# Projecting the queries of the band attention token by token, beside its keys and values

## The chip, the cores and the metric

The kernel runs on one core of a Trainium2 chip. The metric is the time of one execution on the device, in microseconds (us). Before the change three runs took 1618.82, 1613.80 and 1618.34 us, with a median of 1618.34.

## What is computed

One layer of a hybrid encoder, for 2048 prompt frames and 32 frames of a running stream, all in float32:

```python
h = rmsnorm(x, norm_gain)
qa, ka, va, ga, qb, kb, vb, gb = split(h @ w_in)        # 8 x 512 columns
oa = band_attention(qa, ka, va, rel_bias)                # A: 8 heads x 64, own chunk of 64 frames and 8 before
ob = subnorm(diff_attention(rope(qb), rope(kb), vb))     # B: 4 heads of two q/k pairs, block-causal over all frames
y  = rmsnorm(x + concat(oa * silu(ga), ob * silu(gb)) @ w_out, final_gain)
```

Keys and values of the last 512 frames (A) or of all frames (B) are outputs too, as are the rows of the running stream.

## The kernel before

The work is cut into eight **units** of 128 columns of each of q, k, v and gate: four of A (two heads each) and four of B (one head each). They run in the order A, B, B, A, B, A, B, A (line 695). Each unit runs over eight **chunks** of 256 frames (two row tiles of 128). Units on end share nothing but the normalised input, which lies transposed in device memory and is loaded per chunk (tile hT).

Every number is kept as a pair of rounded halves, so that a product is three matmuls: high by high, high by low, low by high. There are two ways to project. `project` (lines 292 to 298) is token-major: 128 frames of hT stand in the array as weights, the columns of w_in stream through, and the result has one frame per partition. `project_T` (lines 300 to 305) has the weights in the array and streams 256 frames: its result is already transposed, one column of w_in per partition. Both take 8 x 3 matmuls. A token-major result is scaled by the frame's norm, a per-partition number in rsd, in the same ACT instruction that takes it out of PSUM (line 349). A transposed result needs the scales along the row: tile rb, 128 equal rows of 256 scales, made in the first unit and loaded by DMA in the others (line 261).

A chunk of **B** projects q, k and v together token-major (384 columns), rotates q and k, and transposes k and q on TensorE (lines 370 and 372) into one PSUM tile tp. A chunk of **A** before the change projects only k and v so (256 columns, twice 24 matmuls), transposes k, and projects q with `project_T` (24 matmuls of 256 columns) into its own PSUM tile qp, which DVE multiplies by rb in place (line 353). From there both go the same way: ACT copies k and q into high parts (lines 382 to 389) and DVE subtracts for the low parts (lines 384 to 391). The gate of both is projected with `project_T` (line 395) and multiplied by rb (line 331). The scores (lines 425 and 426) then go through softmax on DVE, ACT and POOL, are transposed in blocks (line 434), split (lines 443 and 444) and multiplied with the values (lines 547 to 549 and 602 to 603). After the units, the output projection (line 792) uses `project` with 512 columns.

PSUM has two buffers for projections (z_ps), two for transposes (t_ps), three for scores (s_ps), one for outputs (o_ps). The order of the instructions on each engine is fixed when the program is built: a scheduler goes by a modelled timeline and by the priorities that `ahead(n)` gives. TensorE (PE), like the other engines, takes its instructions in that order.

The functions that the change touches are rb_tile, chunk_qkv and subnorm.

Of the kernel before, what the change touches and what calls it, by code (L numbers as in the profile page):

```python
# [8 lines left out]
F32 = mybir.dt.float32  # L9
# [5 lines left out]
P = 128  # L15
# [15 lines left out]
def hybrid_step(  # L31
# [79 lines left out]
    def z_psum():  # L111
        return psum.tile([P, 512], F32, name="z_ps", tag="z", bufs=2)
# [124 lines left out]
    def rb_tile():  # L237
        return pool.tile([P, 256], F32, name="rb", tag="rb", bufs=2)

# [102 lines left out]
    def chunk_qkv(u, isB, c, hR, W, kss, vts):  # L342
        hT, rb = hR
        z = pool.tile([P, 2, 384], F32, name="z", tag="z", bufs=2)
        z0 = 0 if isB else 128
        for tt in range(2):
            zp = z_psum()
            project(hT, tt, W, zp[:, z0:384], slice(z0, 384))
            ACT.activation(z[:, tt, z0:384], zp[:, z0:384], AF.Copy, scale=rsd[:, 2 * c + tt:2 * c + tt + 1])
        if not isB:  # L350
            qp = z_psum()
            project_T(hT, W, qp[:, 0:256], slice(0, 128))
            DVE.tensor_tensor(qp[:, 0:256], qp[:, 0:256], rb, ALU.mult)
        i = u % 4
# [12 lines left out]
        with ahead(150):  # L367
            tp = t_psum()
            for tt in range(2):
                PE.transpose(out=tp[:, tt * P:(tt + 1) * P], in_=z[:, tt, 128:256], identity=ident)  # L370
                if isB:
                    PE.transpose(out=tp[:, 256 + tt * P:256 + (tt + 1) * P], in_=z[:, tt, 0:128], identity=ident)
            if c % 2 == 0:
                kss.append(pool.tile([P, 2, 512], F32R, name="ks", tag="ks", bufs=5))
            ks = kss[c // 2][:, :, (c % 2) * 256:(c % 2 + 1) * 256]
            tk = tp[:, 0:256]
            tq = tp[:, 256:512] if isB else qp[:, 0:256]
            par = parity[0]
# [80 lines left out]
    def subnorm(ob, n, src=None):  # L459
        sq = pool.tile([P, 256], F32, name="sq", tag="sq", bufs=1)  # L460
        op, vp = ob[:, 0:n] if src is None else src, ob[:, 256:256 + n]
        ACT.activation(sq[:, 0:n], op, AF.Square)
        PE.matmul(vp, onesd, sq[:, 0:n], start=True, stop=True)
        rs = pool.tile([P, 256], F32, name="rs", tag="rs", bufs=1)
        ACT.activation(rs[:, 0:n], vp, AF.Ln, bias=eps_t)
        ACT.activation(rs[:, 0:n], rs[:, 0:n], AF.Exp, scale=-0.5)
        on = pool.tile([P, 256], F32, name="on", tag="on", bufs=1)
        DVE.scalar_tensor_tensor(on[:, 0:n], op, gcol[:, 0:1], rs[:, 0:n], ALU.mult, ALU.mult)
        return on
# [400 lines left out]
```

## Time and profile before

| | us |
|---|---|
| three runs, median | 1618.34 |
| the profiled execution, its own time | 1614.23 |
| its span (first to last instruction) | 1612.4 |
| PE busy | 1547.1 |
| DVE busy | 1093.3 |
| ACT busy | 1007.2 |
| POOL busy | 669.3 |

Busy time is the union of an engine's instructions. Matmuls overlap in the pipeline, so the duration of one is longer than what it adds: that is the distance between the starts of neighbours. The clock granted to TensorE was 0.99 of full speed on average. In this trace the units begin (first eviction of their first projection) at 18.5, 159.7, 326.4, 516.7, 699.9, 864.4, 1048.9 and 1214.7 us, in the order given above; the output projection follows from 1400 us on.

### The profile page before, as it was taken

The page shows a single profiled execution, that of the slowest core. Times are in us where ns is not written, and L with a number is a line of the kernel's source. Part 1 is how long each engine was busy: PE and PEld are TensorE (multiplying, and loading weights), DVE is VectorE, ACT ScalarE, POOL GpSimd, SP SyncE. Part 2 cuts the span into 40 slices and gives each one's busy share as a digit, 9 for nine tenths or more (in the row PEclk, how much of TensorE's full clock was granted, in tenths as well). Part 3 has the DMA queues.
Part 4 walks back from the last instruction along what each step waited for, and adds up shares of the span by engine and source line. Part 5 has one row for each costly group of instructions (what it writes and reads, how often), then busy time and mean ns, then how long its engine had stood idle before and what let it go on. Part 6 is the DMA issues. An engine that isn't in the chain of part 4 may idle for free.

```text
span 1612.4 us, 30675 instructions
## 1 busy us (share of the span) xinstructions
PE 1547.1 (96%) x10448; PEld 1430.0 (89%) x10448; DVE 1093.3 (68%) x3045; ACT 1007.2 (62%) x2706; POOL 669.3 (42%) x1117
## 2 busy tenths in 40 slices
PE   7999999999999899999998999999999999989997
PEld 7999999898998899999997999999878899968885
DVE  5777668885788856675788667666888577743333
ACT  7885667785778766655777566556677566531111
POOL 5565424653346534353446344443454344510000
PEclk9999999999999999999999999999999999999999
DMA  9964454433432153336422453354331264334562
GB/s 363 367 231 166 158 192 138 155 107 131 149 128 88 70 196 131 137 131 211 167 83 76 148 181 132 134 180 152 136 131 70 89 248 142 128 133 162 175 211 66
DMA packets 105662, 249.67 MB, mean 155 GB/s; under 512 B 11192, under 2 KB 60480, under 8 KB 88064
## 3 DMA queue, kind: packets, MB, share of 16 engines
q1 hardware_dynamic: 105504, 247.70, 43.3%
q8 instruction: 83, 1.36, 0.3%
q14 instruction: 75, 0.61, 0.1%
HBM read 194.83 MB, written 53.75 MB: 154 GB/s over the span
## 4 chain that ended last, share of the span: by engine, by line
PE 80%; DVE 9%; ACT 4%; issue 3%; DMA 3%; POOL 1%; SPq 0%; DVEq 0%; ACTq 0%; POOLq 0%
PE z_ps L296 12%; PE z_ps L297 12%; PE z_ps L298 12%; PE t_ps L434 6%; PE z_ps L303 5%; PE s_ps L425 5%; PE z_ps L304 5%; PE z_ps L305 5%; PE s_ps L426 5%; PE o_ps L603 2%; PE o_ps L602 2%; DVE nmx L513 2%; PE o_ps L547 2%; PE o_ps L548 2%; PE o_ps L549 2%
## 5 line engine op out<-in xcount | busy, mean ns | idle before, releaser
L296 PE MATMUL z_ps<-w,hT 128*128 128x256 f32 (+2 forms) x1280 | 424.0, 332 | 12.4 <-ACT w L179 6.2
L297 PE MATMUL z_ps<-w,hT 128*128 128x256 f32 (+2 forms) x1280 | 422.4, 330 | 2.0 <-DVE w L180 1.2
L298 PE MATMUL z_ps<-w,hT 128*128 128x256 f32 (+2 forms) x1280 | 421.2, 329 | 0.0
L296 PEld LDWEIGHTS z_ps<-w,hT 128*128 128x128 f32 x1280 | 243.5, 191 | 29.8 <-ACT w L179 6.2
L297 PEld LDWEIGHTS z_ps<-w,hT 128*128 128x128 f32 x1280 | 243.7, 190 | 18.5 <-DVE w L187 2.6
L298 PEld LDWEIGHTS z_ps<-w,hT 128*128 128x128 f32 x1280 | 243.7, 190 | 13.5
L515 ACT ACTIVATE e<-s_ps,nmx 128x512 f32<-128x512 f32 (+3 forms) x320 | 199.0, 626 | 85.1 <-DVE nmx L513 81.2
L444 DVE TENSOR_TENSOR pl<-t_ps,ph 128x512 fp32r<-128x512 f32 (+1 forms) x312 | 191.9, 622 | 77.2 <-ACT ph L443 66.4
L303 PE MATMUL z_ps<-hT,w 128*128 128x256 f32 x768 | 223.3, 291 | 2.8 <-DVE ql L391 2.2
L304 PE MATMUL z_ps<-hT,w 128*128 128x256 f32 x768 | 221.9, 289 | 0.0
L305 PE MATMUL z_ps<-hT,w 128*128 128x256 f32 x768 | 221.2, 288 | 0.0
L443 ACT CAST ph<-t_ps 128x512 fp32r<-128x512 f32 (+1 forms) x312 | 162.4, 535 | 91.2 <-PE o_ps L602 45.9
L425 PE MATMUL s_ps<-ks,qh 128*128 128x512 f32 (+2 forms) x544 | 193.5, 366 | 19.6 <-ACT e L515 17.6
L513 DVE TENSOR_REDUCE nmx<-s_ps 128x1 f32<-128x512 f32 (+3 forms) x320 | 188.2, 600 | 18.9 <-PE s_ps L426 16.0
L426 PE MATMUL s_ps<-ks,ql 128*128 128x512 f32 (+2 forms) x544 | 184.1, 351 | 0.0
L521 POOL TENSOR_SCALAR e<-e,da 128x512 f32<-128x512 f32 (+3 forms) x160 | 111.5, 711 | 140.8 <-DVE da L491 114.9
L303 PEld LDWEIGHTS z_ps<-hT,w 128*128 128x128 f32 x768 | 149.4, 194 | 6.5 <-DVE ql L391 2.9
L304 PEld LDWEIGHTS z_ps<-hT,w 128*128 128x128 f32 x768 | 149.5, 195 | 3.1 <-issue 1.3
L305 PEld LDWEIGHTS z_ps<-hT,w 128*128 128x128 f32 x768 | 149.5, 195 | 1.4
L580 POOL TENSOR_SCALAR ea<-ea,sma 128x640 f32<-128x640 f32 (+4 forms) x128 | 98.2, 769 | 112.8 <-DVE sma L579 99.5
L578 ACT ACTIVATE ea<-ea,nma 128x640 f32<-128x640 f32 (+4 forms) x128 | 97.2, 760 | 61.9 <-DVE nma L576 60.8
L425 PEld LDWEIGHTS s_ps<-ks,qh 128*128 128x128 f32 x544 | 101.8, 189 | 31.9 <-ACT e L515 25.2
(205 smaller groups left out, 3374.9 us busy)
## 6 DMA issues: line engine op xcount, KB each, us to landing
hT<-hTd SPq DMA_DIRECT2D x112, 1024.0 KB, 5.6
wraw<-in_w_in_dram SPq DMA_DIRECT2D x64, 256.0 KB, 5.2
hTd<-hT SPq DMA_DIRECT2D x8, 2048.0 KB, 8.9
oTd<-oT SPq DMA_DIRECT2D x64, 256.0 KB, 3.7
hT<-oTd SPq DMA_DIRECT2D x16, 1024.0 KB, 7.8
out_dram<-z SPq DMA_DIRECT2D x160, 64.0 KB, 1.6
xT<-in_x_t_dram SPq DMA_DIRECT2D x32, 256.0 KB, 5.2
xt<-in_x_prompt_dram SPq DMA_DIRECT2D x32, 256.0 KB, 6.0
```

The costliest lines, as they stand in the source:

```text
L296: PE.matmul(zp, hT[:, 0, k, ts], his[k][:, cols], start=(k == 0), stop=False)
L297: PE.matmul(zp, hT[:, 0, k, ts], los[k][:, cols], start=False, stop=False)
L298: PE.matmul(zp, hT[:, 1, k, ts], his[k][:, cols], start=False, stop=(k == KT - 1))
L303: PE.matmul(zp, his[k][:, cols], hT[:, 0, k, :], start=(k == 0), stop=False)
L304: PE.matmul(zp, his[k][:, cols], hT[:, 1, k, :], start=False, stop=False)
L305: PE.matmul(zp, los[k][:, cols], hT[:, 0, k, :], start=False, stop=(k == KT - 1))
L425: PE.matmul(sp[:, 0:w], QH[:, m, qs], ks[:, m, kc], start=True, stop=False)
L426: PE.matmul(sp[:, 0:w], QL[:, m, qs], ks[:, m, kc], start=False, stop=True)
L443: ACT.copy(out=hv, in_=tv)
L444: DVE.tensor_tensor(lv, tv, hv.bitcast(F32), ALU.subtract)
L513: DVE.tensor_reduce(nmx[:, m, b:b + 1], sp[:, 0:w], AX.X, ALU.max, negate=True)
L515: ACT.activation(e[:, 0:w], sp[:, 0:w], AF.Exp, bias=nmx[:, m, b:b + 1], accum_out=sm[:, m, b:b + 1])
```

## The change

A's q is projected token-major with k and v, as B's is: 384 columns in two times 24 matmuls, one ACT eviction of 384 columns for each row tile that scales all three. The 24 `project_T` matmuls of q and the DVE multiplication by rb go; two transposes for q come, into the second half of tp, and the copies and subtractions for q read them there instead of from qp. The row of scales gets a third buffer. Its space comes from the sub-norm of B, which keeps its result in the tile of squares instead of in one of its own.

```diff
     def rb_tile():
-        return pool.tile([P, 256], F32, name="rb", tag="rb", bufs=2)
+        return pool.tile([P, 256], F32, name="rb", tag="rb", bufs=3)
...
         z = pool.tile([P, 2, 384], F32, name="z", tag="z", bufs=2)
-        z0 = 0 if isB else 128
         for tt in range(2):
             zp = z_psum()
-            project(hT, tt, W, zp[:, z0:384], slice(z0, 384))
-            ACT.activation(z[:, tt, z0:384], zp[:, z0:384], AF.Copy, scale=rsd[:, 2 * c + tt:2 * c + tt + 1])
-        if not isB:
-            qp = z_psum()
-            project_T(hT, W, qp[:, 0:256], slice(0, 128))
-            DVE.tensor_tensor(qp[:, 0:256], qp[:, 0:256], rb, ALU.mult)
+            project(hT, tt, W, zp[:, 0:384], slice(0, 384))
+            ACT.activation(z[:, tt, :], zp[:, 0:384], AF.Copy, scale=rsd[:, 2 * c + tt:2 * c + tt + 1])
...
             for tt in range(2):
                 PE.transpose(out=tp[:, tt * P:(tt + 1) * P], in_=z[:, tt, 128:256], identity=ident)
-                if isB:
-                    PE.transpose(out=tp[:, 256 + tt * P:256 + (tt + 1) * P], in_=z[:, tt, 0:128], identity=ident)
+                PE.transpose(out=tp[:, 256 + tt * P:256 + (tt + 1) * P], in_=z[:, tt, 0:128], identity=ident)
...
-            tq = tp[:, 256:512] if isB else qp[:, 0:256]
+            tq = tp[:, 256:512]
...
-        rs = pool.tile([P, 256], F32, name="rs", tag="rs", bufs=1)
-        ACT.activation(rs[:, 0:n], vp, AF.Ln, bias=eps_t)
-        ACT.activation(rs[:, 0:n], rs[:, 0:n], AF.Exp, scale=-0.5)
+        ACT.activation(sq[:, 0:n], vp, AF.Ln, bias=eps_t)
+        ACT.activation(sq[:, 0:n], sq[:, 0:n], AF.Exp, scale=-0.5)
         on = pool.tile([P, 256], F32, name="on", tag="on", bufs=1)
-        DVE.scalar_tensor_tensor(on[:, 0:n], op, gcol[:, 0:1], rs[:, 0:n], ALU.mult, ALU.mult)
+        DVE.scalar_tensor_tensor(on[:, 0:n], op, gcol[:, 0:1], sq[:, 0:n], ALU.mult, ALU.mult)
```

The scheduler lays the whole program out anew; two places matter below.

**PE, the start of the program.** The end of the first chunk's projection (z_ps_246 and z_ps_272 are its two row tiles) and what follows. Before:

```order
L298 MATMUL z_ps_272<-w_176,hT_179 128x256
L253 MATMUL t_ps_218<-ident_67,rsd_92 128x128
L370 MATMUL t_ps_324<-ident_67,z_245 128x128
L303 MATMUL z_ps_298<-hT_179,w_155 128x256
L304 MATMUL z_ps_298<-hT_179,w_155 128x256
L305 MATMUL z_ps_298<-hT_179,w_155 128x256
```

With the change:

```order
L298 MATMUL z_ps_272<-w_176,hT_179 128x384
L253 MATMUL t_ps_218<-ident_67,rsd_92 128x128
L365 MATMUL t_ps_298<-ident_67,z_245 128x128
L366 MATMUL t_ps_298<-ident_67,z_245 128x128
L303 MATMUL z_ps_424<-hT_179,w_155 128x256
L304 MATMUL z_ps_424<-hT_179,w_155 128x256
L305 MATMUL z_ps_424<-hT_179,w_155 128x256
```

Before, the transposed projections that follow are q's 24 (z_ps_298), then the gate's 24. With the change the gate's come at once (z_ps_424); q is in the 48 matmuls above, each half as wide again.

**PE, the last chunk of the second A unit** (the fourth unit to run). The transposes of its k, and now of its q, and what stands around them. Before, z_ps_10164 is the chunk's q, still being projected when k is transposed:

```order
L303 MATMUL z_ps_10164<-hT_9874,w_7695 128x256
L370 MATMUL t_ps_10194<-ident_67,z_10111 128x128 x2
L603 MATMUL o_ps_9986<-pl_10043,vt_9372 128x256
L602 MATMUL o_ps_9986<-ph_10042,vt_9372 128x256
L603 MATMUL o_ps_9986<-pl_10043,vt_9372 128x256
L304 MATMUL z_ps_10164<-hT_9874,w_7695 128x256
```

With the change (z_ps_10077 is a projection of the next unit):

```order
L298 MATMUL z_ps_10077<-w_9832,hT_9805 128x384
L365 MATMUL t_ps_9790<-ident_67,z_9733 128x128
L366 MATMUL t_ps_9790<-ident_67,z_9733 128x128
L365 MATMUL t_ps_9790<-ident_67,z_9733 128x128
L366 MATMUL t_ps_9790<-ident_67,z_9733 128x128
L596 MATMUL o_ps_9608<-pl_9665,vt_9042 128x256
L595 MATMUL o_ps_9608<-ph_9664,vt_9042 128x256
L596 MATMUL o_ps_9608<-pl_9665,vt_9042 128x256
```

From the last transpose to the first score matmul that reads this chunk's q there now stand 9 projection matmuls of 384 columns, 2 score matmuls of the chunk before (256 columns), 7 value matmuls and 3 transposes. Before, 105 instructions lay between the two, among them the rest of q's projection and the gate's whole one.

## Rows read from the trace of the kernel before

**Rows 1.** The profile's page: busy time and share of each engine; then the mean busy share of the 16 DMA engines in tenths, in 40 slices of 40.3 us.

```profile
PE 1547.1 (96%) x10448; PEld 1430.0 (89%) x10448; DVE 1093.3 (68%) x3045; ACT 1007.2 (62%) x2706; POOL 669.3 (42%) x1117
...
DMA  9964454433432153336422453354331264334562
```

**Rows 2.** Busy time by window, in the middle of the four A units. Columns: window and its length; busy us (and instructions) of PE, PEld (weight loads), DVE, ACT, POOL; granted clock of PE; DMA share, GB/s.

```profile
40.00:160.00 120.00, 118.98 (x943) 115.10 (x943) 88.58 (x304) 93.41 (x260) 73.81 (x115) 1.00 0.69 257
600.00:690.00 90.00, 90.00 (x727) 87.75 (x726) 61.20 (x192) 56.31 (x140) 36.87 (x84) 1.00 0.39 141
950.00:1040.00 90.00, 90.00 (x727) 87.65 (x726) 60.09 (x194) 56.18 (x139) 36.40 (x85) 1.00 0.37 134
1300.00:1390.00 90.00, 90.00 (x725) 87.70 (x724) 66.14 (x205) 55.94 (x140) 41.05 (x90) 1.00 0.47 170
```

**Rows 3.** The same view, 20 us at each of the three changes from a B unit to an A unit.

```profile
500.00:520.00 20.00, 16.14 (x103) 12.98 (x102) 19.29 (x45) 16.49 (x48) 13.48 (x14) 1.00 0.42 152
845.00:865.00 20.00, 16.04 (x93) 12.18 (x92) 19.85 (x43) 16.20 (x46) 15.21 (x17) 1.00 0.42 155
1198.00:1218.00 20.00, 16.15 (x103) 12.99 (x102) 19.29 (x45) 16.50 (x48) 13.49 (x14) 1.00 0.45 152
```

**Rows 4.** The waits of PE over the whole span: who was waited for, us in total, times, longest us.

```profile
PE s_ps L425 <- ACT e L515: 17.6, 18, 2.5
PE z_ps L296 <- ACT w L179: 6.2, 1, 6.2
...
PE z_ps L303 <- DVE ql L391: 2.2, 2, 1.7
```

**Rows 5.** The timeline of PE: first and last matmul of four unbroken runs of projection matmuls. The runs have 24 (56.23 to 58.99) and 28 (634.71 to 638.02) matmuls of 256 columns, 24 and 24 of 384 columns. Columns: start, duration, instruction.

```profile
56.23 0.28 PE L296 MATMUL z_ps<-w,hT 128*128 128x256 f32 x1
...
58.99 0.28 PE L298 MATMUL z_ps<-w,hT 128*128 128x256 f32 x1
...
634.71 0.36 PE L296 MATMUL z_ps<-w,hT 128*128 128x256 f32 x1
...
638.02 0.28 PE L296 MATMUL z_ps<-w,hT 128*128 128x256 f32 x1
...
805.30 0.35 PE L296 MATMUL z_ps<-w,hT 128*128 128x384 f32 x1
...
809.30 0.34 PE L298 MATMUL z_ps<-w,hT 128*128 128x384 f32 x1
...
1067.33 0.42 PE L296 MATMUL z_ps<-w,hT 128*128 128x384 f32 x1
...
1071.43 0.34 PE L298 MATMUL z_ps<-w,hT 128*128 128x384 f32 x1
```

**Rows 6.** The chain that ended last, one piece of it in an A unit: start, us, what.

```profile
91.66 0.77 PE t_ps L434 x7
```

**Rows 7.** Groups of instructions by line and form, over the span: count, busy us in total, mean ns of one; then idle time before them and what ended it.

```profile
L349 ACT ACTIVATE z<-z_ps,rsd 128x384 f32<-128x384 f32 x64 | 37.0, 577 | 11.2 <-PE z_ps L298 10.9
L349 ACT ACTIVATE z<-z_ps,rsd 128x256 f32<-128x256 f32 x64 | 30.1, 470 | 18.9 <-PE z_ps L298 17.8 <-DVE rsd L203 0.5
...
L383 ACT CAST ks<-t_ps 64x256 fp32r<-64x256 f32 x64 | 23.5, 367 | 0.8
L386 ACT ACTIVATE qh<-z_ps 64x256 fp32r<-64x256 f32 x32 | 12.0, 375 | 13.4 <-DVE z_ps L353 13.1
...
L353 DVE TENSOR_TENSOR z_ps<-z_ps,rb 128x256 f32<-128x256 f32 x32 | 13.7, 429 | 10.2 <-PE z_ps L305 9.4
...
L372 PE MATMUL t_ps<-ident,z 128*128 128x128 f32 x64 | 15.9, 273 | 0.0
```

**Rows 8.** The timeline at the start of the program: PE from the end of the first chunk's token-major projection, and the first matmul of the second chunk's (27.62); POOL's low parts of the second chunk's input. In brackets: idle time before and what ended it.

```profile
16.60 0.28 PE L298 MATMUL z_ps<-w,hT 128*128 128x256 f32 x1
17.92 0.32 PE L253 MATMUL t_ps<-ident,rsd 128*128 128x128 f32 x1 [1.04 <-DVE rsd L203]
19.00 0.33 PE L370 MATMUL t_ps<-ident,z 128*128 128x128 f32 x1 [0.76 <-ACT z L349]
19.09 0.36 PE L303 MATMUL z_ps<-hT,w 128*128 128x256 f32 x1
...
26.73 0.52 PE L425 MATMUL s_ps<-ks,qh 128*128 128x256 f32 x3
...
27.62 0.39 PE L296 MATMUL z_ps<-w,hT 128*128 128x256 f32 x1
...
17.81 4.99 POOL L271 TENSOR_TENSOR hT<-xT,hT 128x512 fp32r<-128x512 f32 x4 [3.00 <-ACT hT L270]
```

**Rows 9.** Busy time by window, two of the stretches in which PE was granted half its clock. Columns as in rows 2.

```profile
19.90:23.30 3.40, 3.40 (x19) 3.40 (x18) 1.25 (x3) 2.00 (x8) 3.40 (x5) 0.50 0.95 396
562.60:566.00 3.40, 3.40 (x17) 3.40 (x18) 1.89 (x4) 1.48 (x4) 2.80 (x4) 0.50 0.00 0
```

**Rows 10.** The waits of the DMA queue that SP issues: L261 is the load of the row of scales.

```profile
SPq L261 <- DVE gate L331: 148.4, 19, 24.9
...
SPq L261 <- DVE vt L412: 36.0, 3, 12.1
```

## The prediction

> **What bounds the kernel now.** I read the page first: PE is busy 96% of the span, the next engine, DVE, 68% [rows 1]. An average over stages can hide another bound, so the windows come next. In the middle of the three later A units PE is busy in all of 90 us, and in the first unit in 118.98 of 120, at full clock, with DVE and ACT at 62 to 78% [rows 2]. There only PE's own work counts. In the 20 us where B gives way to A it is different: PE falls to 80% while DVE is busy 96 to 99% [rows 3]; DVE sets the pace there. The waits of PE over the whole span are few and short: 17.6 us for score buffers that ACT has to read, 6.2 us for the first weights, 2.2 us for the buffer that held q until its low part was made [rows 4]. So the change is worth, first, what it does to PE's work in A, and then what it does at the start, at the seams and to the distance between producing q and using it.
>
> **PE's work in a chunk of A.** The cost of a matmul is the distance to the next start, not its duration. For 256 columns the runs give (58.99 - 56.23) / 23 = 0.120 us and (638.02 - 634.71) / 27 = 0.1226; for 384 columns (809.30 - 805.30) / 23 = 0.174 and (1071.43 - 1067.33) / 23 = 0.178 [rows 5]. Before, a chunk has 48 + 24 = 72 matmuls of 256 columns for q, k and v: 72 x 0.120 = 8.64 us. After, 48 of 384: 48 x 0.174 = 8.35 us. That saves 0.29 us (with the slower pair 8.83 - 8.56 = 0.27). Two more transposes cost 2 x 0.77 / 7 = 0.22 us [rows 6]. Net -0.07 us a chunk, -2.2 us over 32 chunks, all of it on the path in the middle of the units. Mixed ends, fast 256 against slow 384 and the reverse, give from +0.12 to -0.26 us a chunk, so +4 to -8 us.
>
> The Trainium skill (TensorE: Matmul & The Clock Gate, Back-to-back issue gap) puts a fixed 2.5 ns beside the columns for each matmul. By that 72 matmuls would take 7.86 us and 48 of them 7.80, so the sum would rise by some 5 us instead of falling by 2.2. The trace shows more than that fixed part: 0.120 us where the page has 0.109.
>
> **ACT and DVE.** ACT's eviction grows from 470 to 577 ns, 64 times: +6.8 us. DVE loses 32 multiplications of 429 ns: -13.7 us [rows 7]. In the middle of the units both hide behind PE [rows 2]; if that cover went, ACT's 6.8 us would count. At the three seams DVE is the bound [rows 3], and I take one multiplication for each: -1.3 us, between 0 (none lies inside) and -2.6 (two each). ACT's copies of q no longer wait for DVE, 13.1 us in all [rows 7]; PE does not wait for those copies there, so nothing comes of it by itself.
>
> **The start of the program.** Before, the 48 matmuls of the first chunk end at 16.60, PE then waits 1.04 and 0.76 us for the row norms, and from 19.09 it does q's and the gate's 48 transposed matmuls, partly at half clock (0.50 from 19.9 to 23.3 [rows 9]); the second chunk's projection starts at 27.62 [rows 8]. After, q's columns ride in the 48 matmuls. They cost 48 x 0.054 = 2.6 us more, which the waits for weights and norms can take up, so they end between 16.6 and 19.2. The gate's 24 take 2.9 us, up to some 5 at half clock. The second chunk's input is ready at 17.81 + 4.99 = 22.80 [rows 8], so its projection can start at 22.8 to 24.5: 3.1 to 4.8 us earlier. About 0.9 us of score matmuls, which came before 27.62, have then still to be done. So -2.2 to -3.9; I take -2.5, nearer the small end, since the 16 DMA engines are busy nine tenths and more until 80 us [rows 1] and the third chunk's input may become the next wait. The other end is 0, if it does at once.
>
> **From z to the scores.** Before, q reached ACT through one DVE operation (0.429). Now its chain is an eviction (0.577), the transposes (four starts, 0.33, and 0.27 to the end of the last) and two copies of k that stand before q's in ACT (0.73) [rows 6, 7]: up to 1.5 us longer. In the last chunk of the second A unit, between the transposes and the first score matmul on this q, the order leaves 9 x 0.174 + 9 x 0.120 + 3 x 0.11 = 3.0 us of PE work [rows 5, 6]. The six copies with the last transpose take 0.27 + 6 x 0.37 = 2.5 us [rows 7] if ACT is free when they come; one softmax instruction in front of them, and PE waits. I take 0.5 us at each of the four unit ends: +2.0 us. The ends are 0 and 1.5 us in every chunk, +47. The row is nearest to the small end: B's chunks have this chain already, and PE's waits in the whole kernel that name q's or k's copies stay below the 2.2 us of the shortest row shown [rows 4].
>
> **At nothing.** The third buffer for the row of scales takes away 148.4 and 36.0 us of waits in SP's queue [rows 10], behind which loads of hT and of weights stand. But the list of PE's waits has none for a DMA, and its longest are others [rows 4], so the cover is hT's own double buffer; were it gone, the one load of weights late at a seam could come sooner, which I leave in the lower end. The sub-norm's tile of squares must now be read by DVE before the next chunk's square is written, a chunk later: nothing. The tile of transposes is held by q's copies as well, some 2 us longer; B's chunks hold it so now.
>
> **Sum.** -2.2 - 1.3 - 2.5 + 2.0 = -4.0 us against the profiled execution's 1614.23: 1610.2. That execution is like the lowest run shown (1613.8), while the median is 4.1 us higher; the four times lie as two pairs with the middle at 1616.3. I forecast the median of such runs: 1616.3 - 4.0 = **1612.3 us**. Its own range is 1607 to 1618.
>
> **Rivals.**
> 1. *Nothing but work.* The earlier start is given back, because the third and fourth chunk wait for their input, and the seams stay with the softmax chain. For it: DMA at nine tenths until 80 us [rows 1], and the seams' DVE time lost is one instruction in some 45 [rows 3]. Against: PE is busy 118.98 of 120 us from 40 us on, so an input that came late did not show there [rows 2]. Left are -2.2 us and a wait or two: about 1615.5.
> 2. *Slower: q comes late.* PE takes its instructions in order, so where the chain of q is not covered the matmuls behind wait too, in the stretches where PE now never waits [rows 2]. In 12 of 32 chunks at 1.48 us that is +17.8, less the 6.0 of gains: 1616.3 + 11.8 = 1628. It decides from about 9 chunks on (9 x 1.48 = 13.3). For it: 3.0 us of cover against 2.5 with ACT at 62% busy. Against: B runs with the same chain and PE still reaches 96%.
> 3. *Faster: the seams heal.* PE loses 3.9 us in each 20 us of the seams [rows 3], 11.6 in all, and the half clock after a wait, as at 562.6 [rows 9], costs 1.7 us each time. A program laid out anew with one PSUM buffer less in use could fill half of it: -8 more, 1604.
> 4. *384 costs in full.* If the 384-column matmuls ran at the slow distance against the fast 256, work rises by 0.12 us a chunk, +3.9 us instead of -2.2: 1618.4. The page named above would have it so; the rows pair fast with fast.
>
> **Chances.** Forecast 0.42, rival 1 0.22, rival 2 0.18, rival 3 0.13, rival 4 0.05. A change of 0.3%, about 4.9 us, is what a measurement of this kernel can tell: faster is below 1613.5, slower above 1623.2. The forecast lies 1.2 us below that line, so some 0.31 of its 0.42 is faster; with rival 3 that is 0.44. Rivals 1 and 4 and the rest of the forecast are the same: 0.38. Slower 0.18. The range runs from 1602 (rival 3 with some of the start's larger gain) to 1626, which takes in half of rival 2.
>
> **What the new profile would show.** PE with 704 matmuls less (768 less, 64 more) and busy some 2 us less; 384-column runs at 0.174 to 0.178 in A; the second chunk's projection from 22.8 to 24.5 us; no line 353; windows in the middle of A still full. Wrong would be: gaps before line 419 that name ACT's copies of q, several tenths of a us in most chunks of A; a PE busy time that rises; or the second chunk still starting near 27 us.

## The result: slower by half a per cent

The changed kernel takes 1625.69 us (median of five runs, 1623.93 to 1628.83) against 1617.85 (five runs, 1613.80 to 1618.82): a ratio of 1.0052, 95% interval 1.0039 to 1.0065. The forecast was 1612.3 in 1602 to 1626. The time lies just inside the range and on the other side of no change. The profiled execution took 1623.93 us, its span is 1622.1.

The page of the changed kernel, as [rows 1]:

```profile
PE 1552.3 (96%) x9744; PEld 1425.7 (88%) x9744; DVE 1088.9 (67%) x3013; ACT 1016.5 (63%) x2706; POOL 666.7 (41%) x1117
...
DMA  9964453242433144335433253345432373234562
```

PE has the 704 matmuls less that were counted, and yet is busy 5.2 us longer. Busy windows of the same places as [rows 2], shifted to where the units now lie (columns as there):

```profile
40.00:100.00 60.00, 59.60 (x408) 58.02 (x407) 44.76 (x160) 54.24 (x157) 38.70 (x58) 1.00 0.90 340
100.00:116.00 16.00, 12.22 (x63) 11.51 (x62) 10.08 (x35) 13.04 (x38) 10.25 (x13) 0.79 0.83 304
...
610.00:700.00 90.00, 90.00 (x625) 87.17 (x624) 58.11 (x193) 57.96 (x138) 37.81 (x79) 1.00 0.37 133
960.00:1050.00 90.00, 90.00 (x628) 86.97 (x627) 59.72 (x197) 58.34 (x141) 37.51 (x78) 1.00 0.41 144
1310.00:1400.00 90.00, 90.00 (x613) 85.96 (x611) 63.93 (x197) 55.73 (x135) 43.00 (x86) 1.00 0.45 166
```

The middle of the later A units is full as before. New is the hole at 100 to 116 us: 12.22 of 16 us, at a mean clock of 0.79. And 20 us at the three seams, as [rows 3]:

```profile
513.00:533.00 20.00, 18.10 (x102) 14.88 (x101) 19.07 (x45) 16.88 (x48) 13.44 (x15) 1.00 0.42 151
855.00:875.00 20.00, 17.41 (x97) 15.20 (x96) 18.22 (x35) 13.94 (x37) 12.96 (x14) 0.91 0.42 152
1209.00:1229.00 20.00, 16.85 (x96) 13.81 (x95) 18.98 (x44) 15.96 (x47) 13.44 (x14) 1.00 0.44 152
```

PE is busy 16.9 to 18.1 us in them instead of 16.1. The list of PE's waits says the same, beside [rows 4]:

```profile
PE s_ps L419 <- ACT e L508: 7.5, 15, 1.7
...
PE s_ps L419 <- ACT qh L381: 3.3, 5, 1.9
...
PE o_ps L595 <- POOL hT L271: 2.7, 1, 2.7
```

B's softmax costs PE 7.5 us where it cost 17.6, and two waits are new.

**A sum of what is lost, unit by unit.** For each matmul I take the distance to the next start less 0.109, 0.119, 0.174 or 0.231 us for 128, 256, 384 or 512 columns (the medians of these distances in the new trace; a few other forms at 0.100), and add these up. This **excess** holds every wait between matmuls and all that the half clock adds. What is left of the span is PE's work at these distances, with some 15 us before the first matmul and after the last: 1503.3 us before, 1503.3 after, and 1503.3 to 1503.8 in the traces of all experiments. It hardly differs because 72 x 0.119 = 8.57 us is also what 48 x 0.174 + 2 x 0.109 gives; with 0.120 for 256 columns the change would save 2.3 us of it. Up to that much, these kernels differ by their excess alone. It is cut at the ACT copy of the last output of each unit (before: at 203.3, 402.8, 591.5, 742.1, 939.6, 1092.3, 1291.2 and 1426.3 us). Units are numbered as they run; `u` is the code's index. Each row is one execution. Where two kernels below have the same order of instructions (units 1 to 6 of the three pairs under "The last unit"), a unit still differs by up to 2.7 us between them, so a smaller difference in one row says nothing.

```
unit (u)         1A(0) 2B(4) 3B(5) 4A(1) 5B(6) 6A(2) 7B(7) 8A(3)  out | sum   | own time | median
before            14.8  14.9  18.6   3.2  19.7   3.3  23.0   2.6   9.1 | 109.0 | 1614.23
after             18.2  21.7  18.7   3.8  21.9   3.0  13.4   9.3   8.8 | 118.8 | 1623.93  | 1625.69
q_alone           22.0  20.5  12.6   5.0  24.0   3.8  13.4   9.1   8.5 | 119.0 | 1624.21  | 1624.57
rb_alone          13.2  20.7  19.5   3.2  18.9   3.0  25.2   2.6   9.4 | 115.7 | 1620.81  | 1621.03
new_but_u0        12.2  18.0  13.7   5.1  22.2   5.5  13.5   9.0   8.8 | 108.1 | 1614.21  | 1613.93
new_u0_only       18.6  22.5  16.7   4.6  12.0   4.8  12.9   4.0   9.7 | 105.6 | 1610.73  | 1610.59
u0_early          14.7  17.3  18.9   3.7  18.4   3.4  20.9   2.6   8.4 | 108.3 | 1613.87  | 1616.04
u0_late           14.4  21.3  16.9   5.0  11.9   4.8  12.1   4.0   9.8 | 100.0 | 1605.26  | 1607.03
new_but_u0late    13.3  17.1  13.4   5.4  22.5   6.1  13.8   8.1   9.0 | 108.6 | 1613.89  | 1613.19
a_gate120         17.7  19.6  18.8   4.1  13.6   6.3  15.8   5.8   9.9 | 111.6 | 1617.20  | 1616.78
u0_u1             18.1  21.2  18.5   3.8  20.7   3.8  20.0   2.8   9.1 | 118.0 | 1623.26  | 1623.98
new_but_u3        17.5  20.3  18.4   3.8  22.0   3.2  21.4   2.6   8.2 | 117.5 | 1622.56  | 1627.68
early_u1_u2       15.4  17.1  12.7   5.1  23.0   3.4  21.2   2.9   9.9 | 110.9 | 1616.00  | 1615.90
a_gate_u3         18.4  21.4  19.0   3.8  21.8   4.9  13.5   7.8   8.7 | 119.4 | 1624.63  | 1626.37
u3_only           13.6  20.7  21.2   3.2  20.7   3.1  15.0   8.0  10.9 | 116.4 | 1621.58  | 1619.98
b_p140            15.9  16.2  22.3   4.9  21.7   3.2  22.9   2.6   9.2 | 119.0 | 1624.24  | 1620.34
b_p160            15.2  15.8  19.7   3.2  19.5   3.4  22.4   3.5   9.0 | 111.6 | 1617.15  | 1617.14
a_p140            20.5  18.7  13.2   5.0  24.8   3.2  14.6   8.9   9.9 | 118.7 | 1623.77  | 1621.97
a_p160            17.5  21.1  18.6   3.8  14.0   5.8  14.0   7.8   8.6 | 111.3 | 1616.87  | 1620.12
```

The whole change is +9.8 us in this sum: +3.4 in the first unit, +6.8 in the second, +2.2 in the fifth (no more than two executions of one order differ by), -9.6 in the seventh, +6.7 in the last, and little elsewhere.

**The first unit.** The start, as [rows 8]; the second chunk's projection begins at 21.89 instead of 27.62:

```profile
16.50 0.34 PE L298 MATMUL z_ps<-w,hT 128*128 128x384 f32 x1
17.31 0.32 PE L253 MATMUL t_ps<-ident,rsd 128*128 128x128 f32 x1 [0.47 <-DVE rsd L203]
18.50 0.33 PE L365 MATMUL t_ps<-ident,z 128*128 128x128 f32 x1 [0.87 <-ACT z L348]
...
18.70 0.36 PE L303 MATMUL z_ps<-hT,w 128*128 128x256 f32 x1
...
21.89 0.42 PE L296 MATMUL z_ps<-w,hT 128*128 128x384 f32 x1
```

At 100 us the excess is 5.5 us, where it was 10.5: the lead of 5 us is still there. Then PE does this, and ACT that:

```profile
105.85 0.34 PE L297 MATMUL z_ps<-w,hT 128*128 128x384 f32 x1
106.03 0.33 PE L298 MATMUL z_ps<-w,hT 128*128 128x384 f32 x1
109.03 0.55 PE L595 MATMUL o_ps<-ph,vt 128*128 128x256 f32 x1 [2.67 <-POOL hT L271]
110.69 0.69 PE L428 MATMUL t_ps<-ident,ea 128*128 128x128 f32 x2 [1.11 <-DVE pl L438]
```

```profile
104.39 0.37 ACT L600 COPY on<-o_ps 64x256 f32<-64x256 f32 x1
104.78 0.63 ACT L216 ACTIVATE junk<-xt 32x512 f32<-32x512 f32 x1
...
105.41 0.61 ACT L246 ACTIVATE xt<-xt 128x512 f32<-128x512 f32 x1
...
107.86 0.61 ACT L216 ACTIVATE junk<-xt 32x512 f32<-32x512 f32 x1
...
108.48 0.93 ACT L437 CAST ph<-t_ps 128x384 fp32r<-128x384 f32 x2
```

PE waits 2.67 us for `o_ps`. The releaser named, POOL's hT, is not one of its operands; ph is, and the first of the two copies that make it, here as one row, ends at 108.93, 0.10 us before PE's restart. Both copies stand in ACT's queue behind six squares of input rows, 104.78 to 108.48. PE takes its matmuls in order, so those behind wait too. Towards the end of this wait the granted clock falls to half:

```profile
108.50:115.30 6.80, 5.17 (x18) 4.91 (x19) 6.67 (x24) 3.94 (x15) 3.46 (x6) 0.50 0.99 403
```

PE is busy for 5.17 us at 1.2 GHz: some 2.6 us lost on top of the waits.

**The last unit.** ACT and PE, 1403.8 to 1408 us:

```profile
1404.12 0.37 ACT L376 CAST ks<-t_ps 64x256 fp32r<-64x256 f32 x1
1404.50 0.37 ACT L377 CAST ks<-t_ps 64x256 fp32r<-64x256 f32 x1
1405.13 0.83 ACT L571 ACTIVATE ea<-ea,nma 128x640 f32<-128x640 f32 x1 [0.26 <-DVE nma L569]
...
1405.96 0.35 ACT L599 COPY on<-o_ps 64x256 f32<-64x256 f32 x1
1406.32 0.36 ACT L600 COPY on<-o_ps 64x256 f32<-64x256 f32 x1
1406.71 0.48 ACT L437 CAST ph<-t_ps 128x384 fp32r<-128x384 f32 x1
1407.09 0.38 ACT L380 ACTIVATE qh<-t_ps 64x256 fp32r<-64x256 f32 x1
1407.47 0.38 ACT L381 ACTIVATE qh<-t_ps 64x256 fp32r<-64x256 f32 x1
```

```profile
1403.82 0.27 PE L366 MATMUL t_ps<-ident,z 128*128 128x128 f32 x1
...
1405.55 0.49 PE L428 MATMUL t_ps<-ident,ea 128*128 128x128 f32 x3
1407.90 0.68 PE L419 MATMUL s_ps<-ks,qh 128*128 128x256 f32 x3 [1.86 <-ACT qh L381]
```

This is the way from z to the scores. ACT is free when the transposes end and copies k at once, but between k's copies and q's stand four instructions of the softmax and of the output before. PE runs out of work at 1406 and waits 1.86 us.

### The profile page after: what moved, and what is told of

It reads as the page before. It is cut to its first block, busy times and chain, and to the rows that moved or that the text cites. A ratio compares the mean times of both kernels' runs of the same rounds, so it can differ in the third digit from the quotient of the medians.

```text
span 1622.1 us, 29163 instructions
## 1 busy us (share of the span) xinstructions
PE 1552.3 (96%) x9744; PEld 1425.7 (88%) x9744; DVE 1088.9 (67%) x3013; ACT 1016.5 (63%) x2706; POOL 666.7 (41%) x1117
## 4 chain that ended last, share of the span: by engine, by line
PE 74%; DVE 11%; ACT 7%; issue 3%; DMA 3%; POOL 2%; SPq 1%; DVEq 0%; ACTq 0%; POOLq 0%
PE z_ps L296 13%; PE z_ps L297 12%; PE z_ps L298 12%; PE t_ps L428 6%; PE s_ps L420 4%; PE s_ps L419 4%; PE z_ps L303 3%; PE z_ps L304 3%; PE z_ps L305 3%; DVE nmx L506 2%; PE o_ps L596 2%; PE o_ps L595 2%; DVE e L519 2%; ACT e L508 2%; PE o_ps L542 1%
## 5 line engine op out<-in xcount | busy, mean ns | idle before, releaser
L296 PE MATMUL z_ps<-w,hT 128*128 128x384 f32 (+1 forms) x1280 | 451.1, 353 | 12.1 <-ACT w L179 6.1
L297 PE MATMUL z_ps<-w,hT 128*128 128x384 f32 (+1 forms) x1280 | 448.8, 351 | 2.9 <-POOL w L184 2.7
L298 PE MATMUL z_ps<-w,hT 128*128 128x384 f32 (+1 forms) x1280 | 447.0, 349 | 0.0
L419 PE MATMUL s_ps<-ks,qh 128*128 128x512 f32 (+2 forms) x544 | 189.3, 370 | 12.5 <-ACT e L508 7.5
L303 PE MATMUL z_ps<-hT,w 128*128 128x256 f32 x512 | 146.8, 287 | 1.1 <-ACT z L348 1.1
L305 PE MATMUL z_ps<-hT,w 128*128 128x256 f32 x512 | 145.7, 285 | 0.0
L304 PE MATMUL z_ps<-hT,w 128*128 128x256 f32 x512 | 145.5, 284 | 0.0
L519 DVE SCALAR_TENSOR_TENSOR e<-e,da 128x512 f32<-128x512 f32 (+2 forms) x96 | 95.9, 1000 | 19.1 <-POOL e L514 18.6
L420 PEld LDWEIGHTS s_ps<-ks,ql 128*128 128x128 f32 x544 | 100.9, 191 | 4.8 <-DVE ql L384 1.2
L337 POOL TENSOR_TENSOR gate<-gate,gabs 128x256 f32<-128x256 f32 (+1 forms) x72 | 51.9, 721 | 127.2 <-ACT gabs L336 127.2
```

What stands on the lines that cost most here:

```text
L296: PE.matmul(zp, hT[:, 0, k, ts], his[k][:, cols], start=(k == 0), stop=False)
L297: PE.matmul(zp, hT[:, 0, k, ts], los[k][:, cols], start=False, stop=False)
L298: PE.matmul(zp, hT[:, 1, k, ts], his[k][:, cols], start=False, stop=(k == KT - 1))
L303: PE.matmul(zp, his[k][:, cols], hT[:, 0, k, :], start=(k == 0), stop=False)
L304: PE.matmul(zp, his[k][:, cols], hT[:, 1, k, :], start=False, stop=False)
L305: PE.matmul(zp, los[k][:, cols], hT[:, 0, k, :], start=False, stop=(k == KT - 1))
```

## The experiments

Every run was timed in three rounds against the kernel before on the same chip; "ratio" is to that kernel. Where the form of q is chosen per unit or chunk, this is the edit of the changed kernel, with another condition in its first line each time:

```diff
+        tokq = isB or u == 0
+        z0 = 0 if tokq else 128
...
-            project(hT, tt, W, zp[:, 0:384], slice(0, 384))
+            project(hT, tt, W, zp[:, z0:384], slice(z0, 384))
...
+        if not tokq:
+            qp = z_psum()
+            project_T(hT, W, qp[:, 0:256], slice(0, 128))
+            DVE.tensor_tensor(qp[:, 0:256], qp[:, 0:256], rb, ALU.mult)
...
-            tq = tp[:, 256:512]
+            tq = tp[:, 256:512] if tokq else qp[:, 0:256]
```

All of these kernels have the third buffer for the scales, also where an expectation calls one "the kernel before".

### The two parts of the change

q's new form with the scales in two buffers as before (q_alone), and the third buffer with q's old form (rb_alone, `tokq = isB`).

```diff
-        return pool.tile([P, 256], F32, name="rb", tag="rb", bufs=3)
+        return pool.tile([P, 256], F32, name="rb", tag="rb", bufs=2)
```

> A's q token-major, but two buffers for the row of scales and the sub-norm's own tile, as before. Theory 1 (moving q costs: its 24 transposed matmuls were filler that PE could put into waits, and its chain to the scores is longer): about 1626, as with the whole change, +8 us against before. Theory 2 (the third buffer for the row of scales lets the next chunks' input work run further ahead and collide on ACT): about 1616, as before or a little below, since the start gains 5 us. Theory 3 (the cost is a matter of the order that the scheduler happens to find): anywhere from 1612 to 1630.

> The kernel before with the third buffer for the row of scales and the sub-norm in the tile of squares, q as before. Theory 1: 1617 to 1618, no change. Theory 2: 1624 to 1628, most of the 8 us and more. Theory 3: a few us either way.

q_alone: 1624.57 us, ratio 1.0042 (1.0027 to 1.0057). rb_alone: 1621.03, ratio 1.0016 (1.0003 to 1.0029). With the new form of q alone most of the loss is there. The third buffer alone touches no work of PE, and yet the second unit's excess rises from 14.9 to 20.7 us in an order laid out anew; its 0.16% are no more than a change of priority moves the time (below).

### Where q's new form costs

In the first unit alone (new_u0_only, `u == 0`), and everywhere but there (new_but_u0, `u != 0`).

> The whole change, except that the first unit (A, where the input is also made) projects q as before. If the loss lies in the first unit (its waits between 100 and 135 us, 6 us, and 3.4 us of half clock): the loss goes and so does the gain of 5 us at the start: 1617 to 1620. If each A unit pays for its longer chain of q: three quarters of the loss stay, 1624. If it is the order alone: anywhere from 1612 to 1630.

> The whole change, but q token-major in the first unit alone, the other three A units as before. If the loss lies in the first unit: 1622 to 1626. If each A unit pays: 1617 to 1620, with the start's gain on top perhaps 1614. If it is the order alone: anywhere from 1612 to 1630.

new_but_u0: 1613.93 us, ratio 0.9976 (0.9965 to 0.9986). new_u0_only: 1610.59, ratio 0.9950 (0.9932 to 0.9967). Each part alone is faster, and together they are slower. new_but_u0 lies in the range for order alone, and new_u0_only below every range. So the new form has no price per unit of A that could be added up. In the table new_u0_only has the loss in its first unit (18.6), and gets it back in units 5 and 7, where B runs with unchanged code: 12.0 and 12.9 instead of 19.7 and 23.0.

### How much the order alone is worth

The same instructions, with the priority of the copies of k and q a little lower or higher, in the kernel before (b_p140, b_p160) and in the changed one (a_p140, a_p160).

```diff
-        with ahead(150):
+        with ahead(140):
```

> The kernel before with one number changed that computes nothing: the priority of the transposes and copies of k and q, 150, is 140. The same instructions in another order. If the order that the scheduler happens to find is worth several us: away from 1618 by 3 to 10 us, to either side. If the order hardly matters and the change itself costs: 1616 to 1620.

> The same with 160, which moves a third as many instructions. If the order is worth several us: away from 1618 by 2 to 8 us, perhaps the other way than 140. If it hardly matters: 1616 to 1620.

> The changed kernel with 140 for 150. If the order is worth several us: away from 1625 by 3 to 10 us, to either side, so that it may meet the kernel before. If the change itself costs: 1623 to 1628, clearly above both variants of the kernel before.

> The changed kernel with 160 for 150. If the order is worth several us: away from 1625 by 3 to 10 us, to either side. If the change itself costs: 1623 to 1628.

Ratios: b_p140 1.0022 (1.0004 to 1.0040), b_p160 0.9998 (0.9985 to 1.0011), a_p140 1.0024 (1.0011 to 1.0038), a_p160 1.0013 (1.0000 to 1.0025). With the two kernels themselves the old form gives 1.0000, 1.0022 and 0.9998, the new one 1.0052, 1.0024 and 1.0013. The order alone is worth some 4 us in the old form and 6 in the new (0.0024 and 0.0039 of the time). The new form is worse on average, by some 0.2%, but the two sets of three overlap, and a single pair says little. In three places of the table the two sets of three do not overlap: the first unit (14.8 to 15.9 us with the old form, 17.5 to 20.5 with the new), the seventh (22.4 to 23.0, and 13.4 to 14.6) and the last (2.6 to 3.5, and 7.8 to 9.3).

### The first unit: an early start and no cover

New form in chunks 0 to 3 of the first unit alone (u0_early), in its chunks 4 to 7 alone (u0_late), and everywhere but in these last four (new_but_u0late).

```diff
+        tokq = isB or (u == 0 and c < 4)
```
```diff
+        tokq = isB or (u == 0 and c >= 4)
```
```diff
+        tokq = isB or u != 0 or c < 4
```

> The kernel before, with q projected token-major in the first four chunks of the first unit alone. Theory 1 (the loss in the first unit arises because q's 24 transposed matmuls of a later chunk are no longer there to run while ACT and DVE are late at 100 to 116 us): the start's gain stays (second chunk's projection near 22 us instead of 27.6) and the waits at 100 to 116 us do not come, since chunk 4 has its old form: the first unit ends 3 to 6 us earlier than before (near 198 to 200 us by its last output) instead of 4.3 us later, and if the units behind it keep their lengths the time is 1612 to 1615. Theory 2 (the scheduler's new order alone decides, and has nothing to do with the form of q): the end of the first unit lies anywhere within 5 us of before, and the time anywhere from 1611 to 1626.

> The kernel before, with q projected token-major in the last four chunks of the first unit alone: the complement of the run with the first four. Theory 1: no gain at the start (second chunk's projection near 27.6 us), and the waits of PE with the half clock behind them at 100 to 116 us come as in the whole change, so the first unit ends 5 to 9 us later than before (208 to 212 us by its last output): 1621 to 1627 if the units behind it keep their lengths. Theory 2 (order alone): no such tie between the form of chunk 4 and the waits at 100 to 116 us; anywhere from 1611 to 1626.

> The whole change, except that the last four chunks of the first unit keep the old form. Theory 1: the first unit ends 5 to 9 us earlier than with the whole change (198 to 203 us), PE without the waits at 100 to 116 us; if the units behind keep their lengths the time is 1617 to 1620, near no change. Theory 2 (order alone): anywhere from 1611 to 1626, the first unit's end with it.

The changed kernel with the gate's projection of A at a lower priority (a_gate120):

```diff
-        with ahead(-30):
+        with ahead(-30 if isB else -120):
```

> The whole change, and the 24 transposed matmuls of A's gate get a lower priority (-120 instead of -30), so that they stand later in PE's order and can run where q's did. Theory 1: PE again has independent matmuls while ACT and DVE are late, so the excess over the pitch in 100 to 116 us falls from 9 to below 4 us, and the time to 1617 to 1621. Theory 2 (order alone): the excess there need not fall; anywhere from 1611 to 1628.

Excess from the start of the program to a time in us:

```
                  30    60   100   116   130   150   175   200
before           8.9   9.8  10.5  10.6  11.4  11.4  11.7  14.5
after            4.0   4.9   5.5  12.1  13.1  14.3  17.3  17.3
new_u0_only      4.2   5.2   5.8  12.4  13.8  14.9  17.9  17.9
u0_early         3.5   4.4   6.7   8.3   9.6   9.6   9.9  14.2
new_but_u0late   3.7   4.6   6.8   8.5   9.7   9.7  10.1  12.8
u0_late          8.4   9.2   9.3   9.3  10.8  10.8  13.9  13.9
a_gate120        4.4   4.4   5.0   6.1  13.1  13.1  15.1  15.7
```

The window 100 to 116 us in the kernel before, then u0_early, u0_late, and a_gate120 with the next 14 us:

```profile
100.00:116.00 16.00, 16.00 (x135) 15.91 (x134) 10.92 (x36) 13.29 (x38) 7.88 (x13) 1.00 0.55 198
```
```profile
100.00:116.00 16.00, 14.94 (x120) 14.28 (x119) 10.27 (x35) 14.74 (x41) 11.60 (x16) 1.00 0.79 288
```
```profile
100.00:116.00 16.00, 16.00 (x112) 15.73 (x111) 11.30 (x39) 14.68 (x43) 10.44 (x13) 1.00 0.63 222
```
```profile
100.00:116.00 16.00, 15.24 (x107) 14.75 (x106) 10.77 (x35) 13.50 (x40) 9.76 (x13) 1.00 0.53 180
116.00:130.00 14.00, 10.81 (x60) 9.10 (x60) 10.94 (x36) 8.68 (x23) 8.38 (x17) 0.76 0.85 318
```

The lead of 4 to 5 us comes with the new form in the first chunks, each time. With the new form in chunks 4 to 7 as well, 6.6 us go at 100 to 116; with the old form there, 1.6 to 1.7 and no half clock. But u0_late, new in chunks 4 to 7 and without the lead, loses nothing in that window. The expectation had the waits come there, so the cause as I had put it falls: it takes **both**, PE ahead of ACT's input work and q's 24 transposed matmuls gone from the order. In u0_late the gate's 24 of a chunk still lie in the window (101.3 to 106.0 us); the whole change has done them by 99.5. The other traces agree: 5.5 to 6.8 us go there in all eight that have lead and new form, a_gate120 set aside, and q_alone, without the third buffer, is one of them; 1.6 to 1.7 in the three with the lead alone, and at most 0.3 in the seven without it. u0_early keeps its lead to 175 us (9.9 against 11.7) and has lost it at 200 us, against an expected 3 to 6 us. A second loss, 2.0 to 3.1 us from 150 to 175, comes in the four kernels here with new late chunks, u0_late among them, and in none of the other three. In three of the four it is mainly one wait of 1.55 us for the output buffer, which DVE has still to read.

The gate's matmuls put later fill the window, as expected, and the hole comes 15 us later with the same 7 us. The time of a_gate120, 1616.78 (ratio 0.9994, 0.9983 to 1.0005), lies at the lower edge of the first theory's 1617 to 1621, but for another reason: its units 5 and 8 lose 8.3 and 3.5 us less than those of the whole change.

Times: u0_early 1616.04 (0.9996, 0.9983 to 1.0009), u0_late 1607.03 (0.9933, 0.9913 to 0.9952), new_but_u0late 1613.19 (0.9962, 0.9946 to 0.9977). The times of u0_early and new_but_u0late miss theory 1, and u0_late lies below both of its ranges. u0_late beats both kernels, but by units 5 and 7 (11.9 and 12.1), not by the unit that was edited.

### The last unit

Three pairs that have the same order of instructions up to 1200 to 1209 us, where the last A unit's first projection joins the last B unit: the whole change without and with the last A unit in the new form (new_but_u3 and after), the same pair with the old form at the end of the first unit (early_u1_u2 and new_but_u0late), and all units in the old form without and with the last (rb_alone and u3_only).

```diff
+        tokq = isB or u != 3
```
```diff
+        tokq = isB or (u != 3 and (u != 0 or c < 4))
```
```diff
+        tokq = isB or u == 3
```

> The whole change, except that the last A unit keeps the old form. The order of instructions is that of the whole change up to the last B unit. Theory 1 (the tail loses because in the last unit nothing is left to run while ACT makes the high parts of k and q): the last unit's excess over the pitch falls from 9.3 to 2.6 to 4.0 us, and the wait of 2.0 us before the first scores of the last chunk goes; with the last B unit unchanged the time is 1618 to 1621. Theory 2 (the order alone, not the form of q): the last unit keeps 6 us of its excess or the last B unit rises by as much, 1623 to 1628.

> The new form in the first four chunks of the first unit and in the second and third A unit; old form in the last four chunks of the first unit and in the last A unit. Against the kernel that had the last A unit new as well (1613.2 us) only the order from the last B unit on differs. Theory 1: the last unit's excess falls from 8.1 to 2.6 to 4.0, the time to 1607 to 1610, which is faster than both kernels. Theory 2: no fall, 1612 to 1616.

> The kernel with the third buffer for the scales and the old form of q everywhere except in the last A unit. Up to the last B unit its order is that of the kernel with the third buffer alone (1621.0 us). Theory 1 (both effects belong to q's form in the last A unit): the last B unit's excess over the pitch falls from 25 to 13 to 15 us, the tail's rises from 2.6 to 8 to 9.5, together 4 to 6 us less: 1615 to 1618. Theory 2 (both came from what was changed in front): no such pair of changes, 1619 to 1628.

In all three pairs the last unit's excess is higher with the new form: 9.3 against 2.6, 8.1 against 2.9, 8.0 against 2.6 us. In all three the B unit in front gains more than that: 13.4 against 21.4, 13.8 against 21.2, 15.0 against 25.2. The last unit behaved as expected; the B unit did not for the first two, and I had left that side out. The third pair was expected to show both, and did, but its time, 1619.98, lies above the 1615 to 1618 that I took from it. The window 1385 to 1412 us of the whole change, then of new_but_u3:

```profile
1385.00:1412.00 27.00, 24.75 (x151) 22.01 (x150) 24.16 (x65) 16.98 (x44) 16.95 (x32) 0.94 0.29 103
```
```profile
1385.00:1412.00 27.00, 27.00 (x195) 25.26 (x194) 21.74 (x57) 14.82 (x37) 15.09 (x27) 1.00 0.33 119
```

With the old form PE is busy all the time there, with 44 matmuls more, and never waits. What stands behind the last chunk's transposes in new_but_u3 is its gate's projection:

```profile
1397.53 0.38 PE L371 MATMUL t_ps<-ident,z 128*128 128x128 f32 x2
...
1398.57 0.29 PE L303 MATMUL z_ps<-hT,w 128*128 128x256 f32 x1
...
1402.69 0.28 PE L305 MATMUL z_ps<-hT,w 128*128 128x256 f32 x1
1402.81 0.28 PE L426 MATMUL s_ps<-ks,qh 128*128 128x256 f32 x1
```

All 24 lie between 1398.57 and 1402.69, after q's own 24, and matmuls of the output projection follow. In the whole change the gate's 24 (1385.76 to 1389.64) and 33 matmuls of the output projection have run before the transposes at 1403.48. So there was other work; the order laid out anew has it too early.

Nine kernels have q's new form in the last unit, and eight of them the same wait of 1.86 us. In five (after, new_but_u0late, q_alone, a_p140, new_but_u0) a half clock of 3.4 us begins during it or within 1.1 us of its end; in three (u3_only, a_p160, a_gate_u3) none comes. The ninth, a_gate120, does not have the wait, with the same form of q: there 13 matmuls of the output projection (512 columns) stand between the last transpose and the first scores on this q, and ACT has one instruction instead of four between k's copies and q's.

```profile
1396.11 0.27 PE L366 MATMUL t_ps<-ident,z 128*128 128x128 f32 x1
...
1400.85 0.39 PE L296 MATMUL z_ps<-w,hT 128*128 128x512 f32 x1
1401.08 0.45 PE L419 MATMUL s_ps<-ks,qh 128*128 128x256 f32 x2
```

So it need not be q's own 24 matmuls that stand there: others cover the chain as well, and the order decides whether they do. Times: new_but_u3 1627.68 (1.0062, 1.0040 to 1.0083), early_u1_u2 1615.90 (0.9985, 0.9969 to 1.0000), u3_only 1619.98 (1.0021, 1.0011 to 1.0031). None of the pairs shows a clear gain from the old form at the end, since the seam in front takes it.

The whole change with the gate's matmuls later in the last unit alone (a_gate_u3):

```diff
-        with ahead(-30):
+        with ahead(-120 if u == 3 else -30):
```

> The whole change, with the gate's 24 transposed matmuls at a lower priority in the last A unit alone, so that they can stand between the scores of the last chunks as q's did before. All that comes before the last chunks keeps its order. Theory 1: the tail's excess falls from 9.3 to 3 to 6 us and the time to 1619 to 1623. Theory 2 (the cover does not matter there): no fall, 1624 to 1627.

The last unit's excess falls from 9.3 to 7.8 us, the time is 1626.37 (1.0054, 1.0034 to 1.0074): a miss. The last of the gate's 24 matmuls in the last chunk, and the wait:

```profile
1391.92 0.28 PE L305 MATMUL z_ps<-hT,w 128*128 128x256 f32 x1
...
1410.04 0.68 PE L419 MATMUL s_ps<-ks,qh 128*128 128x256 f32 x3 [1.86 <-ACT qh L381]
```

The edit did not do what it was meant for: the gate's 24 still stand some 14 us ahead of the transposes (1405.63), the wait is the same 1.86 us, and the fall of 1.5 us is the half clock that did not come. It says nothing of whether they would cover the wait.

### From one unit to two

> The new form in the first and second A unit, the old one in the third and fourth: the next step from the first unit alone, which took 1610.6 us, towards the whole change, 1625.7. Theory 1 (an inner unit of A costs nothing, its chain being covered by the B unit behind it; only first and last lose): 1609 to 1613. Theory 2 (the order laid out anew decides at the seams): the two B units behind the second A unit go back from 12 to 18 to 25 us of excess each, and the time to 1616 to 1624.

`tokq = isB or u <= 1` adds the second A unit to new_u0_only: 1623.98 us, ratio 1.0050 (1.0036 to 1.0065), against 0.9950. The sum rises by 12.4 us, of which the edited unit 4 has none; 8.7 and 7.1 come in units 5 and 7. The wait of PE for B's softmax in new_u0_only, then in u0_u1:

```profile
PE s_ps L426 <- ACT e L515: 7.1, 14, 0.9
```
```profile
PE s_ps L426 <- ACT e L515: 13.9, 23, 2.0
```

So the second theory holds here: the same B code waits twice as long in another order. A B unit with the seam behind it has 12 to 16 us of excess in some orders and 17 to 25 in others. At the last seam the form of q behind it decides in the three pairs; what decides at units 3 and 5 was not found.

## Why the prediction was wrong

- **PE's work, -2.2 us: mis-sized, it is near 0.** The mean distance in unbroken projections at full clock is 0.1194 us for 256 columns before and 0.1745 for 384 after: 72 x 0.1194 = 8.60 us, and 48 x 0.1745 + 2 x 0.109 = 8.59. By an estimate with the formula of the Trainium skill (TensorE: Matmul & The Clock Gate, Back-to-back issue gap), which the page gives for an isolated matmul, it would have risen by some 5 us; the trace has neither a rise nor the saving. PE's busy time rose by 5.2 us without more work: the profile counts what the half clock adds as busy, and the first part of each wait, since a matmul's duration is longer than its distance to the next. The stretches at half clock hold 0.9 us of the rise, the beginnings of waits (93 instead of 77) 3.1. I had named a rise as a sign of being wrong without that way to it.
- **The start, -2.5 us: right as a step, wrong as a gain.** It brought 5.7 us at the second chunk and 5.0 at 100 us, more than the upper end, also because the half clock of 19.9 to 23.3 us [rows 9], worth 1.7, did not come again. Rival 1 had it given back, by DMA, by the third or fourth chunk. It was given back from 106 us on, when the seventh chunk was being projected, to ACT, which does the input's squares and casts at its own pace. I had no term for what ACT has to do in the first unit. I read PE's full window up to 160 us [rows 2] as a sign that no input was late. It was full because PE was late itself and had q's and the gate's 48 matmuls to run.
- **The seams, -1.3 us: one healed.** In the 20 us shown PE idles 4.0 us less in all, but by whole units the seventh lost 9.6 us less, the third the same, the fifth 2.2 more. One DVE instruction less is not what does it: new_u0_only has both late seams low with the old q behind them. Rival 3 was the right kind of case, for one seam of three, and worth more there than its whole -8.
- **From z to the scores, +2.0 us: the step that failed.** It took 0.5 us at each of four ends. Where a B unit's projection stands behind there is none to see: units 4 and 6 have 3.8 and 3.0 us of excess, before 3.2 and 3.3. At the last end the unit cost 5.2 to 6.7 us more in the pairs. I had 3.0 us of cover against 2.5 of copies, with one softmax instruction in front at worst. There PE had work for 2.0 us behind the transposes (to 1406.0), and q's copies came 3.8 us behind them (1407.85), with four instructions of ACT, 2.0 us, between k's copies and q's. Rival 2 had this mechanism, in twelve chunks at 1.48 us; the wait sits in one place and is 1.86 us. The rest of the 6.7 is a half clock behind it, in two of the three pairs, and shorter waits, one of 1.06 us for the output buffer.
- **What no term had.** Matmuls that depend on nothing were counted as 2.9 us of work. They were also what PE did while ACT was late, and taking them away costs where the order has nothing else to run. And a change of order moves units whose code is the same: the second unit costs 6.8 us more; rb_alone has 5.8 of it without any change to q, and q_alone 5.6 without the third buffer. I had written moved loads and buffers at nothing and kept a rival only for orders that heal. This failed too.

The sum as it came out: 0 for work, -5.0 by 100 us, +8.4 in the rest of the first unit, +6.8 in the second, +2.2 in the fifth, -9.6 in the seventh, +6.7 in the last, +0.1 for the rest: +9.6, beside 9.7 between the two profiled executions and 7.8 between the medians. The forecast was also counted from 1616.3, the middle of two pairs of times, 1.5 us below the median that five runs then gave. Shown by experiment are the first unit's conjunction, and that in three pairs the loss in the last unit and the gain at the seam in front of it come with q's form there; a_gate120, which has the form without the wait, shows that the order laid out for it brings the wait and not the form by itself. Why the second unit is slower, and why units 3 and 5 are sometimes 5 to 9 us better, is open.

## What to carry to other kernels

When a change takes independent work out of an in-order engine, ask what that engine did with it: find the places where another engine is late, above all the first and the last stretch, and price the wait there and the half clock that may come with it. A head start on one engine is worth only what the next-slowest engine in that stretch can follow. In a program that a scheduler lays out anew, measure how much a meaningless change of priority moves the time, here 4 to 6 us, before giving a smaller effect a cause.

## What the runs showed of the hardware

A half clock can come with a short wait, but not each time. In the changed kernel PE had been busy for 59.60 of the 60 us up to 100; 2.1 us into a wait of 2.67 us (106.4 to 109.0) the granted clock fell, and PE ran at 1.2 GHz from 108.5 to 115.3 us, which cost some 2.6 us. The same wait of 1.86 us in the last unit had a half clock of 3.4 us in or just behind it in five kernels and none in three. Matmuls of 256 and 384 columns with a weight load each lie 0.119 and 0.174 us apart at full clock, nearly in the ratio of their columns (0.68 for 0.67): a third fewer, wider matmuls saved nothing.
